# A hybrid decoder layer on one core: more sevenfold chunks in the down projection, their right-hand sums made partly in DRAM

## Chip, core and metric

The kernel runs on one core of a Trainium2 chip. The metric is the device time of one execution in microseconds; 2% is about what a measurement of this kernel can tell from no change.

## The reference

One decoder layer on 256 tokens of width 2048 in float32. A mixer joins a gated recurrence (RG-LRU) and a sliding-window attention with sinks (32 query heads, 4 key heads of 64), an output projection follows, and then an MLP with hidden width 8192. Cut to what matters:

```python
h = rmsnorm(x, norm_mix_pre[l])
proj = h @ w_in[l]                               # xr, yr, q, k, v and two gates
...
scores = jnp.einsum('bnqhgd,bnkhd->bnhgqk', qb, kk).astype(jnp.float32)
...
mix = sigmoid(g_rnn) * (y_rnn @ w_rnn_proj[l]) + sigmoid(g_attn) * (y_att @ w_attn_proj[l])
x = x + rmsnorm(mix @ w_out[l], norm_mix_post[l])
h = rmsnorm(x, norm_mlp_pre[l])
u = jnp.square(jax.nn.relu(h @ w_mlp_up[l]))     # 2048 -> 8192
x = x + rmsnorm(u @ w_mlp_down[l], norm_mlp_post[l])   # 8192 -> 2048
```

## The kernel before

**Three products for one.** Every weight and activation is split into a high part in the reduced-precision type fp32r and a low part, what the rounding left. A product is three matmuls: high by high, high by low, low by high (`product`, L905 to L908).

**The stream.** All weights come through one `Stream`: 1 MiB chunks of 128x2048 float32, in halves of 1024 columns. The SP queue loads a half into one of four raw buffers (L73), ScalarE copies the high part (`whi`, L91), VectorE subtracts to get the low part (`wlo`, L92), and TensorE uses both. There are six buffers of each part, and the splits are written six halves ahead of use. The order of the program text sets the order; a scheduler then places each engine's instructions.

**The MLP.** The hidden width is done in two halves f = 0, 1. The up phase of a half makes 16 blocks of hidden columns (`a_pair`, L234 for the high part of the weights, L237 for the low), each from two chunks. `evacuate` squares them. The down phase follows (`down`), two passes n = 0, 1 over 1024 output columns each, 16 chunks p = 0 to 15 a pass, in eight banks of PSUM: four that exist only for the sevenfold products (`P1`, `P6`, `Q5`, `N7`, in two two-bank tiles `s0` and `s1` that the up phase uses too) and four `P2`, `Q3`, `Q4`, `Cs`.

**Sevenfold chunks.** A chunk p covers 2x2 blocks of weights and 2x2 of activations. Done plainly, that is 8 block products, 24 matmuls of 128x512. For p in `SEVEN` = 0, 2, 4, ..., 12 it is done in 7 block products (Strassen's scheme in Winograd's form), 21 matmuls. It needs sums of the blocks on both sides. The left-hand sums are made once when the hidden block is evacuated (`seven`). The right-hand sums of the weights are made in each pass by VectorE in `split_sums` (L104, L106, L107), and need a split of their own (L110 on ScalarE, L111 on VectorE). Seven chunks in four passes are 28.

**Scores.** `attention` computes the scores of the four heads of one parity, which lie on 64 partitions, into one bank (two banks where the keys are 256 wide), and then those of the other parity, on the other 64 partitions (L527); VectorE empties each bank (L532).

Of the kernel before, what the change touches and what calls it, by code (L numbers as in the profile page):

```python
# [34 lines left out]
WRAW, WHALF, T2, HELD = 4, 6, 8, 4  # L35

SEVEN = (0, 2, 4, 6, 8, 10, 12)
PAIRS = 16
# [13 lines left out]
class Stream:  # L52
# [3 lines left out]
    def __init__(self, nc, pool, chunks, room, sums):  # L56
        self.nc, self.pool, self.chunks, self.room, self.sums = nc, pool, chunks, room, sums
        self.raw, self.parts = {}, {}
        self.loaded = self.split = 0
        self.pin = lambda i: i  # L60
        self.at = 0

    def load_to(self, n):
        while self.loaded < min(n, 2 * len(self.chunks)):
            j = self.loaded
            c = slice(j % 2 * 1024, j % 2 * 1024 + 1024)
            if j < 2 * EXTRA:
                if j % 2 == 0:
                    self.place = self.room(f"wraw{j}")
                t = self.place[:, c]  # L70
            else:
                t = self.pool.tile([P, 1024], F32, tag="wraw", bufs=WRAW, name=f"wraw{j}")
            self.nc.sync.dma_start(t, self.chunks[j // 2][:, c])  # L73
            self.raw[j] = t
            self.loaded += 1

    def split_to(self, n):
        while self.split < min(n, 2 * len(self.chunks)):
            j = self.split
            if j // 2 in self.sums:  # L80
                self.split_sums(j)
                self.split += 2
                continue
            self.load_to(j + 1)
            self.parts[j] = self.two_parts(self.raw.pop(j), j)
            self.split += 1

    def two_parts(self, src, j):
        hi = self.pool.tile([P, 1024], F32R, tag="whi", bufs=WHALF, name=f"whi{j}")
        lo = self.pool.tile([P, 1024], F32R, tag="wlo", bufs=WHALF, name=f"wlo{j}")  # L90
        self.pin(self.nc.scalar.copy(hi, src))  # L91
        self.pin(self.nc.vector.tensor_tensor(lo, src, hi.bitcast(F32), ALU.subtract))  # L92
        return hi, lo

    def split_sums(self, j):


        self.load_to(j + 2)
        v = self.nc.vector
        a, b = self.raw.pop(j), self.raw.pop(j + 1)  # L100
        t = self.room(f"t{j}")[:, 0:1536]
        hi, lo = [self.room(f"t{part}{j}").bitcast(F32R)[:, 0:1536] for part in ("hi", "lo")]
        one, two, l, r = t[:, 0:1024], t[:, 1024:1536], slice(0, 512), slice(512, 1024)
        v.tensor_tensor(one.rearrange("p (a b) -> p a b", a=2), b[:, l].unsqueeze(1).to_broadcast([P, 2, 512]),  # L104
                        a.rearrange("p (a b) -> p a b", a=2), ALU.add)
        v.tensor_tensor(b[:, l], t[:, l], a[:, r], ALU.add)  # L106
        v.tensor_tensor(two, b[:, l], b[:, r], ALU.add)  # L107
        ahi, alo = self.two_parts(a, j)
        bhi, blo = self.two_parts(b, j + 1)
        self.nc.scalar.copy(hi, t)  # L110
        v.tensor_tensor(lo, t, hi.bitcast(F32), ALU.subtract)  # L111
        parts = {"B11": (ahi[:, l], alo[:, l]), "B22": (ahi[:, r], alo[:, r]), "T2": (bhi[:, l], blo[:, l]),
                 "B21": (bhi[:, r], blo[:, r])}
        for i, name in enumerate(("T1", "T3", "T4")):
            c = slice(i * 512, i * 512 + 512)
            parts[name] = hi[:, c], lo[:, c]
        self.parts[j] = parts

    def ahead(self, j):
        self.split_to(j + AHEAD)  # L120
        self.load_to(max(2 * EXTRA, j + WHALF) + WRAW)

    def half(self, run_ahead=True):
        j = self.at
        self.at += 1
        if run_ahead:
            self.ahead(j)
        else:
            self.split_to(j + 1)
        return self.parts.pop(j)  # L130

    def seven(self):

        j = self.at
        self.at += 2
        self.ahead(j)
        return self.parts.pop(j)
# [4 lines left out]
AHEAD = 6  # L142
HELD_LAST = 5
# [6 lines left out]
def layer(tc, x, pos_t, pos_row, inv_freq, vecs, sinks, gains, w_kv, w_q, w_xy, w_rg, w_g, w_rp, w_ap, w_out,  # L150
# [9 lines left out]
    pairs = [psa, psa]  # L160

# [22 lines left out]
    chunks += [w_out[i] for i in range(16)]  # L184
    sums = set()
    for f in range(2):
        chunks += [w_up[32 * f + i] for i in range(32)]
        for n in range(2):
            sums.update(len(chunks) + i for i in SEVEN)
            chunks += [w_dn[(2 * f + n) * PAIRS + i] for i in range(PAIRS)]  # L190

# [6 lines left out]
    ws = Stream(nc, wpool, chunks, lambda name: flat(unit(name, F32)), sums)  # L198
# [25 lines left out]
    def a_pair(acts, out):  # L224
# [3 lines left out]
        for f in range(2):  # L228
            both = ps[:, f].rearrange("p a b -> p (a b)")
            for half in range(2):  # L230
                hi, lo = ws.half()
# [4 lines left out]
                for k, a in enumerate(act):  # L236
                    mm(ps[:, f, 1, :], lo[:, k * P : k * P + P], a[:, 0, :], start=False,  # L237
                       stop=half == 1 and k == 7)
# [889 lines left out]
```

## Time and profile before

| | us |
|---|---|
| runs | 1554.41, 1555.5, 2158.74 (median 1555.5) |
| profiled execution | 1553.58 |
| its span | 1551.8 |
| TensorE busy | 1525.7 (98%) |
| VectorE busy | 1117.5 (72%) |
| ScalarE busy | 843.9 (54%) |
| GpSimd busy | 1.7 |
| high parts, L91, 528 instructions | 549.0 |
| low parts, L92, 528 instructions | 639.8 |

The span is what the profiler recorded between the first and the last instruction; 1.8 us lie around it. Busy times of different engines overlap. The up phases run from 850 to 1030 us and from 1197 to 1375, the down phases from 1030 to 1197 and from 1375 to 1543. In rows of the profile PE is TensorE, PEld its weight load, DVE VectorE, ACT ScalarE, POOL GpSimd and SP the queue that loads the weights; L908 is line 908 of the kernel.

### The profile page before, as it was taken

Reading aid. Unit: us, or ns where it says so; the run is one execution under the profiler, and the core shown is the slowest. Engines: PE = TensorE matmul, PEld = TensorE weight load, DVE = VectorE, ACT = ScalarE, POOL = GpSimd, SP = SyncE. Lnnn points to the kernel's source line nnn. Section 1 sums busy time; section 2 is a strip of 40 time slices with the busy share of each in tenths; the row PEclk is TensorE's granted clock in tenths of the full one; section 3 lists DMA queues with packets and bytes.
Section 4 is the critical chain, followed back from the end, with each engine's and each line's share of the span. In section 5 each row is a group of like instructions: output and inputs, shape, how many; then the busy total and the mean of one; then the engine's idle time right before and its main releaser. Section 6 shows DMA issues by size and latency. Waiting matters only on the chain.

```text
span 1551.8 us, 20974 instructions
## 1 busy us (share of the span) xinstructions
PE 1525.7 (98%) x8042; PEld 1295.5 (83%) x8042; DVE 1117.5 (72%) x1364; ACT 843.9 (54%) x1156; POOL 1.7 (0%) x9
## 2 busy tenths in 40 slices
PE   8999999999999999999999999999999999999997
PEld 6887777888888888888787888888888888888885
DVE  6666666866859877555655866688886666788997
ACT  5555545646647766444344655555454555555553
POOL 0000000000000000000000000000000000000000
PEclk9999999999999999999999999999999999999999
DMA  6554354354655465555663855556666655566664
GB/s 246 188 169 148 115 173 147 124 191 149 229 188 177 158 213 198 190 184 190 250 221 98 278 190 189 187 175 213 218 203 218 221 187 189 188 242 232 203 216 138
DMA packets 82902, 296.26 MB, mean 191 GB/s; under 512 B 9585, under 2 KB 9841, under 8 KB 81777
## 3 DMA queue, kind: packets, MB, share of 16 engines
q1 hardware_dynamic: 79344, 285.48, 55.7%
q10 hardware_dynamic: 3458, 9.45, 1.6%
q8 instruction: 63, 1.03, 0.3%
q14 instruction: 37, 0.30, 0.1%
HBM read 288.60 MB, written 6.29 MB: 190 GB/s over the span
## 4 chain that ended last, share of the span: by engine, by line
PE 87%; DVE 5%; ACT 3%; DMA 3%; issue 2%; SPq 0%; DVEq 0%; ACTq 0%
PE ps L234 36%; PE ps L237 18%; PE dQ L908 7%; PE s L908 4%; PE dP L908 3%; DVE wlo L92 2%; PE dCs L908 2%; DMA wraw<-in_w_dn 2%; PE o L251 2%; PE o L255 2%; PE o L253 2%; PE q L251 2%; PE q L253 2%; PE q L255 2%; PE sc L527 1%
## 5 line engine op out<-in xcount | busy, mean ns | idle before, releaser
L92 DVE TENSOR_TENSOR wlo<-wraw,whi 128x1024 fp32r<-128x1024 f32 x528 | 639.8, 1221 | 322.4 <-ACT whi L91 317.0
L91 ACT CAST whi<-wraw 128x1024 fp32r<-128x1024 f32 x528 | 549.0, 1049 | 585.9 <-PE ps L234 271.5
L234 PE MATMUL ps<-hT,whi 128*128 128x512 f32 x1024 | 260.5, 394 | 0.0
L234 PE MATMUL ps<-h2T,whi 128*128 128x512 f32 x1024 | 258.2, 394 | 0.5 <-DVE h2T L280 0.5
L234 PEld LDWEIGHTS ps<-hT,whi 128*128 128x128 f32 x1024 | 183.8, 189 | 36.5 <-issue 3.5
L234 PEld LDWEIGHTS ps<-h2T,whi 128*128 128x128 f32 x1024 | 185.3, 190 | 34.2 <-DVE h2T L280 0.9
L237 PEld LDWEIGHTS ps<-hT,wlo 128*128 128x128 f32 x1024 | 140.1, 190 | 11.7 <-issue 2.0
L237 PEld LDWEIGHTS ps<-h2T,wlo 128*128 128x128 f32 x1024 | 140.0, 191 | 10.1
L237 PE MATMUL ps<-hT,wlo 128*128 128x256 f32 x1024 | 145.3, 283 | 0.0
L237 PE MATMUL ps<-h2T,wlo 128*128 128x256 f32 x1024 | 143.0, 283 | 0.0
L908 PE MATMUL dQ<-whi,uT 128*128 128x512 f32 x288 | 106.5, 389 | 0.0
L234 PE MATMUL ps<-yrnn,whi 128*128 128x512 f32 x256 | 64.4, 393 | 0.7 <-DVE yrnn L700 0.7
L234 PE MATMUL ps<-yatt,whi 128*128 128x512 f32 x256 | 64.1, 392 | 0.0
L908 PEld LDWEIGHTS dQ<-whi,uT 128*128 128x128 f32 x288 | 54.1, 188 | 11.2
L908 PE MATMUL dQ<-wlo,uT 128*128 128x512 f32 x144 | 56.1, 390 | 1.6 <-DVE wlo L92 1.6
L111 DVE TENSOR_TENSOR tlo<-t,thi 128x1536 fp32r<-128x1536 f32 x28 | 49.2, 1757 | 10.1 <-ACT thi L110 10.1
L908 PE MATMUL dP<-whi,uT 128*128 128x512 f32 x144 | 53.8, 389 | 0.0
L908 PE MATMUL dCs<-whi,uT 128*128 128x512 f32 x144 | 53.7, 389 | 0.0
L234 PEld LDWEIGHTS ps<-yrnn,whi 128*128 128x128 f32 x256 | 46.0, 189 | 9.3 <-DVE yrnn L700 1.1
L234 PEld LDWEIGHTS ps<-yatt,whi 128*128 128x128 f32 x256 | 46.0, 189 | 8.2
L251 PE MATMUL q<-whi,hT 128*128 128x512 f32 x128 | 51.1, 399 | 0.0
L253 PE MATMUL q<-wlo,hT 128*128 128x512 f32 x128 | 50.2, 392 | 0.0
(251 smaller groups left out, 2068.6 us busy)
## 6 DMA issues: line engine op xcount, KB each, us to landing
wraw<-in_w_up SPq DMA_DIRECT2D x128, 512.0 KB, 4.6
wraw<-in_w_dn SPq DMA_DIRECT2D x128, 512.0 KB, 4.5
wraw<-in_w_g SPq DMA_DIRECT2D x64, 512.0 KB, 4.4
wraw<-in_w_xy SPq DMA_DIRECT2D x64, 512.0 KB, 3.9
wraw<-in_w_q SPq DMA_DIRECT2D x32, 512.0 KB, 4.3
wraw<-in_w_ap SPq DMA_DIRECT2D x32, 512.0 KB, 3.8
wraw<-in_w_rp SPq DMA_DIRECT2D x32, 512.0 KB, 4.6
wraw<-in_w_out SPq DMA_DIRECT2D x32, 512.0 KB, 4.8
```

Of the source, the lines that this page charges most:

```text
L91: self.pin(self.nc.scalar.copy(hi, src))
L92: self.pin(self.nc.vector.tensor_tensor(lo, src, hi.bitcast(F32), ALU.subtract))
L111: v.tensor_tensor(lo, t, hi.bitcast(F32), ALU.subtract)
L234: mm(both, hi[:, k * P : k * P + P], a.rearrange("p a b -> p (a b)"), start=half == 0 and k == 0, stop=False)
L237: mm(ps[:, f, 1, :], lo[:, k * P : k * P + P], a[:, 0, :], start=False, stop=half == 1 and k == 7)
L251: mm(banks[tb][n], a[:, 0, t], hi[:, n * 512 : n * 512 + 512], start=first, stop=False)
L253: mm(banks[tb][n], a[:, 0, t], lo[:, n * 512 : n * 512 + 512], start=False, stop=False)
L255: mm(banks[tb][n], a[:, 1, t], hi[:, n * 512 : n * 512 + 512], start=False, stop=last)
L527: mm(ps[:, i * w : i * w + w], qT[r0 : r0 + HD, h, tb * P : tb * P + P], kT[r0 : r0 + HD, g, 0:w], start=True, stop=True)
L908: mm(b, a[x], w[y], start=not begun and i == 0, stop=tail and i == 2)
```

## The change

There are seven parts.

1. **42 sevenfold chunks.** `SEVEN` becomes a table for each half f: ten chunks a pass for f = 0 and eleven for f = 1, so 2 × 10 + 2 × 11 = 42. Chunk 0 is plain in every pass.
2. **Sums in DRAM.** For 28 of the 42, GpSimd's queue makes the four right-hand blocks in a DRAM tile: three copies and three accumulating transfers, 2 MiB written for a chunk. A step is issued with every sixth piece that isn't of the down weights. The other 14 (`MAKE`: p = 2, 6, 10, 13 for f = 0, p = 2, 5, 9 for f = 1) are made by VectorE.
3. **Pieces for halves.** The stream works in pieces of up to 2048 columns: two raw buffers (two more from the pool `big` at the start and in the down phases), three pairs of high and low parts. A sevenfold chunk is two pieces: a, three blocks of the weights (1536 columns), loaded; and b, the four sums (2048 columns), loaded from DRAM or made. The products follow them, three blocks and then four.
4. The last `a_pair` of an up phase is emptied with priority.
5. **Scores.** The products of the two parities alternate, each parity in its own bank.
6. Three (f = 0) or four (f = 1) of the `seven` tiles lie in the pool `big`.
7. In the last pass `x1` is loaded later, the gain `g3` comes before the pass on ScalarE's queue, and its products with `acc` are made after chunks 2 to 5.

```diff
-WRAW, WHALF, T2, HELD = 4, 6, 8, 4
-SEVEN = (0, 2, 4, 6, 8, 10, 12)
+T2, HELD = 8, 2
+SEVEN = ((1, 2, 3, 5, 6, 7, 9, 10, 11, 13), (1, 2, 3, 4, 5, 7, 8, 9, 10, 11, 12))
+MAKE = ((2, 6, 10, 13), (2, 5, 9))
+IN_UNITS = (3, 4)
...
+            if self.pieces[j][0] is None and c.start == 0:
+                self.make(src, self.free(j - 1))
+            hi, lo = self.parts[j]
+            i = self.pin(self.nc.scalar.copy(hi[:, c], src[:, c]))
+            self.pin(self.nc.vector.tensor_tensor(lo[:, c], src[:, c], hi[:, c].bitcast(F32), ALU.subtract))
...
+    def make(self, t, w):
         v = self.nc.vector
+        q = [slice(i * 512, i * 512 + 512) for i in range(4)]
+        v.tensor_tensor(t[:, 0:1024].rearrange("p (a b) -> p a b", a=2), w[:, q[3]].unsqueeze(1).to_broadcast([P, 2, 512]),
+                        w[:, 0:1024].rearrange("p (a b) -> p a b", a=2), ALU.add)
+        v.tensor_tensor(t[:, q[2]], t[:, q[0]], w[:, q[1]], ALU.add)
+        v.tensor_tensor(t[:, q[3]], t[:, q[2]], w[:, q[2]], ALU.add)
...
+PARTS, RAW = 3, 2
+EVERY = 6
...
+                    if i in MAKE[f]:
+                        pieces.append((piece(src)[0], 1536, 2048, own(at)))
+                        pieces.append((None, 2048, 2048, own(at + 1)))
+                    else:
+                        t = away.tile([P, 2048], F32, name=f"sums{len(ahead_of)}")
+                        ahead_of.append((t, src))
+                        pieces.append(piece(src, 1536, 2048, own(at)))
+                        pieces.append(piece(t, 2048, 2048, own(at + 1)))
...
+            if i >= 2:
+                t, w = ahead_of[i - 2]
+                dma(t[:, 1536:2048], t[:, 1024:1536], accum_op=ALU.add)
+            if 1 <= i <= len(ahead_of):
+                t, w = ahead_of[i - 1]
+                dma(t[:, 1024:1536], t[:, 0:512], accum_op=ALU.add)
+            if i < len(ahead_of):
+                t, w = ahead_of[i]
+                dma(t[:, 0:512], w[:, 1536:2048])
+                dma(t[:, 512:1024], w[:, 1536:2048])
+                dma(t[:, 1024:2048], w[:, 512:1536])
+                dma(t[:, 0:1024], w[:, 0:1024], accum_op=ALU.add)
+            yield step
...
+        if j % EVERY == 0 and j >= EVERY and pieces[j][0] and pieces[j][0][0][1].tensor.name != w_dn.tensor.name:
+            for d in next(summing, ()):
+                tc.add_manual_dep(d.ins, i.ins.name, after, reason="a step of the sums")
...
-            for par in range(2):
-                r0 = par * HD
-                for j in range(4 // per):
-                    ps = bank(psm, "sc")
-                    for i in range(per):
-                        h = j * per + i
-                        mm(ps[:, i * w : i * w + w], qT[r0 : r0 + HD, h, tb * P : tb * P + P],
+            for j in range(4 // per):
+                both = [bank(psm, "sc") for par in range(2)]
+                for i in range(per):
+                    h = j * per + i
+                    for par in range(2):
+                        r0 = par * HD
+                        mm(both[par][:, i * w : i * w + w], qT[r0 : r0 + HD, h, tb * P : tb * P + P],
                            kT[r0 : r0 + HD, g, 0:w], start=True, stop=True)
...
+    LEFT = {"P1": (0, 0), "Q3": (6, 1), "P2": (2, 2), "Q5": (4, 0), "N7": (3, 1), "P6": (5, 2), "Q4": (1, 3)}
...
-            a_pair(h2T, wide(u))
+            a_pair(h2T, wide(u), PRIO if p == PAIRS - 1 else 0)
```

Three places show what the new text makes of the engines' order. The first is TensorE in the attention: the scores of one group (`sc` are the banks, `kT` and `qT` the keys and queries), before and then now; `ps` and `q10` are other projections.

```order
L527 MATMUL sc_912<-kT_428,qT0_816 128x128 x4
L527 MATMUL sc_919<-kT_428,qT0_816 128x128 x4
...
L527 MATMUL sc_1064<-kT_428,qT0_816 128x256 x2
L527 MATMUL sc_1069<-kT_428,qT0_816 128x256 x2
L251 MATMUL q10_1077<-whi32_888,hT0_138 128x512
```

```order
L582 MATMUL sc_900<-kT_437,qT0_813 128x128
L582 MATMUL sc_901<-kT_437,qT0_813 128x128
L582 MATMUL sc_900<-kT_437,qT0_813 128x128
L582 MATMUL sc_901<-kT_437,qT0_813 128x128
...
L582 MATMUL sc_1021<-kT_437,qT0_813 128x256 x2
L582 MATMUL sc_1046<-kT_437,qT0_813 128x256 x2
L307 MATMUL q10_1059<-whi16_934,hT0_166 128x512
L582 MATMUL sc_1047<-kT_437,qT0_813 128x256 x2
```

The 128-wide products alternate between two banks. The 256-wide of this group stay in twos of one bank; in two of the four groups one pair of banks alternates.

The second is TensorE where the first down phase opens, before and then now; `ps` is the last up block.

```order
L237 MATMUL ps_9007<-h2T3_6759,wlo335_8945 128x256 x4
L908 MATMUL s0_9110<-whi336_8972,seven00_7781 128x512
L908 MATMUL s0_9110<-wlo336_8973,seven00_7781 128x512
L908 MATMUL s0_9110<-whi336_8972,seven00_7781 128x512
L908 MATMUL dQ3_9113<-whi336_8972,seven00_7781 128x512
...
L908 MATMUL dQ4_9114<-thi336_8967,seven00_7781 128x512
L908 MATMUL s1_9111<-thi336_8967,seven00_7781 128x512
```

```order
L290 MATMUL ps_8636<-h2T3_6535,wlo167_8591 128x256 x4
L971 MATMUL dQ3_8722<-whi168_8637,uT00_7182 128x512
L971 MATMUL dQ3_8722<-wlo168_8638,uT00_7182 128x512
L971 MATMUL dQ3_8722<-whi168_8637,uT00_7182 128x512
...
L971 MATMUL dCs_8724<-wlo168_8638,uT00_7182 128x512
L971 MATMUL dCs_8724<-whi168_8637,uT00_7182 128x512
L971 MATMUL s0_8719<-whi169_8674,seven01_7495 128x512
```

The two-bank tiles `s0` and `s1` were needed with the first and the sixteenth matmul of the phase; now 24 matmuls of a plain chunk come ahead of the first that needs them.

The third is VectorE where it makes sums: before, chunk 4 of the first pass and the plain one behind it, and now p = 3, 4 and 5 of the first pass of f = 1 (pieces 257 to 262, made from 261 into 262).

```order
L104 TENSOR_TENSOR t344_9163<-wraw345_9116,wraw344_9086 128x1024
L92 TENSOR_TENSOR wlo344_9170<-wraw344_9086,whi344_9169 128x1024
L106 TENSOR_TENSOR wraw345_9116<-t344_9163,wraw344_9086 128x512
L107 TENSOR_TENSOR t344_9163<-wraw345_9116 128x512
L92 TENSOR_TENSOR wlo345_9174<-wraw345_9116,whi345_9173 128x1024
L92 TENSOR_TENSOR wlo346_9217<-wraw346_9147,whi346_9216 128x1024
L92 TENSOR_TENSOR wlo347_9221<-wraw347_9149,whi347_9220 128x1024
L111 TENSOR_TENSOR tlo344_9165<-t344_9163,thi344_9164 128x1536
```

```order
L103 TENSOR_TENSOR wlo257_11390<-wraw257_11321,whi257_11389 128x1536
L103 TENSOR_TENSOR wlo258_11406<-wraw258_11324,whi258_11405 128x2048
L103 TENSOR_TENSOR wlo259_11423<-wraw259_11371,whi259_11422 128x1536
L103 TENSOR_TENSOR wlo260_11439<-wraw260_11374,whi260_11438 128x2048
L117 TENSOR_TENSOR wraw262_11409<-wraw261_11393 128x1024
L103 TENSOR_TENSOR wlo261_11458<-wraw261_11393,whi261_11457 128x1536
L119 TENSOR_TENSOR wraw262_11409<-wraw262_11409,wraw261_11393 128x512
L120 TENSOR_TENSOR wraw262_11409<-wraw262_11409,wraw261_11393 128x512
L103 TENSOR_TENSOR wlo262_11471<-wraw262_11409,whi262_11470 128x2048
```

A made sum was followed by the parts of a plain chunk ahead of its own last part; now two chunks without adds stand ahead of the three adds, and the part of piece 262 directly behind them. GpSimd, which issued no transfers, now issues all those of part 2.

More of the change, by code (lines that the diff above doesn't have):

```diff
@@ L119, in ahead, with load @@
[L119 to L123, printed above, removed]
+        self.each = lambda j, i: None
+        self.waits = [0, 0]
+    def load(self):
+        if self.loaded == len(self.pieces):
+            return False
+        j = self.loaded
+        loads, w, step, own = self.pieces[j]
+        if self.waits[own] == (EXTRA if j < EXTRA else RAW):
+            return False
+        t = self.room(f"wraw{j}") if own else self.pool.tile([P, 2048], F32, tag="wraw", bufs=RAW, name=f"wraw{j}")
+        for c, src in loads or ():
+            self.nc.sync.dma_start(t[:, c], src)
+        self.raw[j] = t
+        self.waits[own] += 1
+        self.loaded += 1
+        return True
@@ L124, in half, with ahead, next @@
+    def ahead(self, last):
+        self.split_to(sum(j <= last for j, c in self.cuts))
+        while self.load():
+            pass
+    def next(self, run_ahead=True):
         j = self.at
         self.at += 1
[L126 to L136, printed above, removed]
+        self.ahead(j + PARTS - 1 if run_ahead else j)
         return self.parts.pop(j)
```

303 lines of the change are left out of this document (152 added, 151 removed).

## The prediction

> **What bounds the kernel now.** I read the page's totals first, then the chain, the waits, and the work stage by stage.
>
> ```profile
> PE 1525.7 (98%) x8042; PEld 1295.5 (83%) x8042; DVE 1117.5 (72%) x1364; ACT 843.9 (54%) x1156; POOL 1.7 (0%) x9
> PE 87%; DVE 5%; ACT 3%; DMA 3%; issue 2%; SPq 0%; DVEq 0%; ACTq 0%
> ACT whi L91 <- PE ps L234: 271.5, 195, 4.1
> DVE wlo L92 <- ACT whi L91: 317.0, 294, 3.0
> ```
>
> TensorE is busy for 98% of the span and carries 87% of the chain that ended last. The two largest waits show the direction: the split of a weight into high and low part starts on ScalarE when TensorE gives a buffer back, and VectorE follows ScalarE. The feeders wait for TensorE, so only matmul time comes off the end, and a feeder costs something only once it is late.
>
> ```profile
> core 0: us, PE busy (x) PEld busy (x) DVE busy (x) ACT busy (x) POOL busy (x), PEclk, DMA share, GB/s
> 850.00:1030.00 180.00, 180.00 (x1024) 158.23 (x1023) 132.79 (x166) 104.31 (x140) 0.00 (x0) 0.99 0.62 205
> 1030.00:1197.00 167.00, 166.21 (x736) 137.44 (x736) 138.18 (x132) 85.56 (x82) 0.00 (x0) 1.00 0.62 209
> 1197.00:1375.00 178.00, 178.00 (x1023) 156.69 (x1022) 124.17 (x147) 97.09 (x119) 0.00 (x0) 1.00 0.60 195
> 1375.00:1543.00 168.00, 165.26 (x728) 135.90 (x726) 144.94 (x148) 84.43 (x92) 0.00 (x0) 1.00 0.64 215
> ```
>
> The rows are the up and down phases of the two halves of the hidden layer. TensorE is full in all four, and the clock is at 0.99 to 1.00, so nothing is to be had from the clock. In the down phases VectorE is at 83% and 86% already: it is the feeder with the least left. The profiled execution took 1553.6 us (span 1551.8 and 1.8 around it), 0.1% under the median of 1555.5. The sum below starts from 1553.6.
>
> **(a) Fewer products.** A plain chunk needs 24 matmuls, a sevenfold one 21. With 42 sevenfold chunks for 28, 14 × 3 = 42 matmuls of 128x512 go.
>
> ```profile
> 1447.98 2.72 PE dQ L908 x12
> 999.99 1.84 PE ps L234 x8
> 1001.83 0.95 PE ps L237 x8
> ```
>
> In the chain twelve down matmuls take 2.72 us, 0.227 each: 42 × 0.227 = −9.5 us. The same price gives what is needed later: a plain chunk holds TensorE for 5.44 us, a sevenfold one for 4.76, now in two pieces, a (9 matmuls, 2.04) and b (12, 2.72). An up chunk is 2 × (1.84 + 0.95) = 5.58.
>
> **(b) Scores.** The two head parities lie on the upper and lower 64 partitions; their products now alternate between two banks.
>
> ```profile
> L527 PE MATMUL sc<-kT,qT 64*128 64x256 f32 x64 | 17.0, 396 | 0.0
> L527 PE MATMUL sc<-kT,qT 64*128 64x128 f32 x64 | 6.8, 285 | 0.0
> L567 PE MATMUL po<-pT,v_sb 128*64 128x512 f32 x32 | 7.7, 605 | 0.0
> L339 PE MATMUL gain_b<-gain,ones 128*128 128x512 f32 x8 | 3.7, 609 | 0.3 <-DMA gain<-in_gains 0.3
> ```
>
> No row shows 64-row products side by side. The nearest do so for columns: the 32 po records, which use 64 columns each and alternate between the halves, hold TensorE for 7.7/32 = 0.24 us each, the full-width records of the same length 3.7/8 = 0.46. So two halves did run together, and I take half the time where the instructions really alternate. In the changed order all of the 128-wide products alternate, but of the 256-wide only those of the second bank pair in two of the four groups, a quarter: −6.8/2 − 17.0/8 = −5.5 us. Bounds: 0 if nothing overlaps, −11.9 if all does.
>
> The Trainium skill's "TensorEngine Tiling (Array Packing)", section "Performance Considerations", says against this that tiling speeds up the matmuls but not what empties PSUM. The row on it in this trace is the next one, VectorE's emptying of the score bank: TensorE waited for it once, 0.4 us. By the rule taken fully this term would be 0 and the sum 1555; the trace speaks for the row.
>
> ```profile
>   DVE s L532: 0.4, 1
> ```
>
> **(c) Opening of the down phase.** Today it opens with a sevenfold chunk, whose products need the two-bank tile that the last up chunk still occupies.
>
> ```profile
> 1034.94 0.50 PE L908 MATMUL s<-thi,seven 128*128 128x512 f32 x1 [0.79 <-DVE u L241]
> 1379.68 0.50 PE L908 MATMUL s<-thi,seven 128*128 128x512 f32 x1 [1.12 <-DVE u L241]
> ```
>
> These are TensorE's gaps of 0.79 and 1.12 us. A plain chunk first gives 5.44 us of work in other banks, and the last up tile is emptied with priority: −1.9 us (0 if another wait takes the place).
>
> **(d) Sums on VectorE.** Fourteen sevenfold chunks still make their sums there, and now without half the buffers: three pairs of high and low parts, each a whole piece.
>
> ```profile
> L92 DVE TENSOR_TENSOR wlo<-wraw,whi 128x1024 fp32r<-128x1024 f32 x528 | 639.8, 1221 | 322.4 <-ACT whi L91 317.0 <-issue 3.6 <-PE ps L237 0.7
> L111 DVE TENSOR_TENSOR tlo<-t,thi 128x1536 fp32r<-128x1536 f32 x28 | 49.2, 1757 | 10.1 <-ACT thi L110 10.1
> L104 DVE TENSOR_TENSOR t<-wraw,wraw 128x1024 f32<-128x1024 f32 x28 | 34.2, 1223 | 9.9 <-DMA wraw<-in_w_dn 9.2 <-PE dQ L908 0.3
> L106 DVE TENSOR_TENSOR wraw<-t,wraw 128x512 f32<-128x512 f32 x28 | 19.2, 684 | 0.1
> L107 DVE TENSOR_TENSOR t<-wraw 128x512 f32<-128x512 f32 x28 | 19.3, 691 | 0.9
> L91 ACT CAST whi<-wraw 128x1024 fp32r<-128x1024 f32 x528 | 549.0, 1049 | 585.9 <-PE ps L234 271.5 <-DVE wraw L106 66.7 <-issue 52.3
> L110 ACT CAST thi<-t 128x1536 fp32r<-128x1536 f32 x28 | 41.4, 1479 | 14.6 <-DVE t L107 8.3 <-PE s L908 6.2
> ```
>
> No row has 2048 columns; one step further from 1024 and 1536 gives 1.76 + 0.54 = 2.29 us on VectorE and 1.48 + 0.43 = 1.91 on ScalarE. A chunk whose sums VectorE makes costs it 1.22 + 0.68 + 0.69 + 1.76 + 2.29 = 6.64 us against 4.76 of TensorE, 1.88 too much; one whose sums come from DRAM 4.05, a plain one 2.29 against 5.44. On average VectorE keeps up, but it may be only three pieces ahead. Take p = 5 of the second half, after two DRAM chunks. Time 0 is when TensorE has done piece a of p = 3. ScalarE and VectorE split piece b of p = 4 (1.91, 2.29: 4.20), then VectorE does three adds and the low part of piece a (4.35: 8.55); piece b of p = 5 is copied (10.46) and subtracted (12.75). TensorE has b, a, b, a before it: 2.72 + 2.04 + 2.72 + 2.04 = 9.52. It stalls 3.2 us. So does p = 9, in both passes: 4 × 3.2 = +12.9 us. The other ten follow a plain chunk among the last two (10.20 + 2.04 = 12.24 against 12.75, or more room): 0.5 us each at most, within the overlap of neighbouring instructions, taken as 0. Bounds: 0, and 14 × 1.88 = 26.3.
>
> The 14 additional (pass, chunk) places are 7 more chunks whose activations are spread into seven; their added VectorE work (three small subtractions and three more column blocks) lies in the up phases, where VectorE idles for about 50 us each: 0.
>
> **(e) Loads in the down phase.** A DRAM chunk loads 0.75 + 1 MiB (1.835 MB) in 4.76 us: 385 GB/s wherever such chunks follow each other.
>
> ```profile
> 16.00:22.00 6.00, 5.77 (x22) 4.55 (x21) 4.53 (x8) 3.40 (x10) 0.00 (x0) 0.62 1.03 411
> 1375.00:1400.00 25.00, 23.88 (x107) 19.43 (x106) 16.87 (x17) 12.22 (x13) 0.00 (x0) 1.00 0.87 318
> wraw<-in_w_dn SPq DMA_DIRECT2D x128, 512.0 KB, 4.5
> ```
>
> The fullest stretch moved 411 GB/s; the second row, 318 at a share of 0.87, makes 366 when full. At 366 a DRAM chunk takes 5.01 us, 0.25 more than TensorE: 28 × 0.25 = 7 us at most. I take 0: runs are two or three long, and a plain chunk or a stall of (d) follows each. A transfer lands 4.5 us after its issue, which two pieces ahead cover.
>
> **(f) Sums in DRAM.** GpSimd's queue, idle today, issues a step each six pieces, mostly before the down phases: 1 MiB copied and 1 MiB added, with the reading of the old value about 3 MiB of traffic, on the transfer engines that carry the weights. On average it fits: six up pieces (6.29 MB) and a step (3.15) are 9.44 MB in 6 × 5.58 = 33.5 us, 282 GB/s. At 366 GB/s one step is 8.6 us. If all of it went ahead of the loads, the split pieces in hand cover 2 × 5.58 − (1.91 + 2.29) = 6.96 us, and 1.6 us stay uncovered: 0 to 28 × 1.6 = 45 us. I take 0, since the loads are issued in the same time and share the engines. The two raw buffers in front also count: a load of 5 us, copy and subtraction make 9.2 us for two chunks of 11.2, so a load may be 2 us late.
>
> **Sum.** 1553.6 − 9.5 − 5.5 − 1.9 + 12.9 = 1549.6, given as 1550 us.
>
> **The rivals.**
> 1. *VectorE is never late.* If the adds slip into VectorE's waits for ScalarE, (d) is 0: 1553.6 − 16.9 = 1537 us, with all scores halved 1530. For it: VectorE waited 317 us for ScalarE. Against it: the adds stand in order behind the subtraction of the piece before.
> 2. *The down phases become feeder-bound*, on the other side of the time before. It decides from the point where VectorE, at 83 to 86% today, has no slack that it can use before a made sum, and DRAM chunks run at 366 GB/s: 1553.6 − 16.9 + 26.3 + 7 = 1570 us. Against it: ten of the made sums stand near a plain chunk.
> 3. *GpSimd's transfers starve the weights.* It decides once a step holds up a load by more than 6.96 us: 1549.6 + 45 = 1594 us, with TensorE gaps each six pieces in the up phases. For it: the transfer engines are at 0.60 to 0.62 there without any steps. The Trainium skill's "DMA: Bandwidth & Descriptors", section "Issuing engines are not separate DMA queues", states that transfers from different engines end on the same 16 and interleave; by that rule the delay is shared, not whole, and no run here has shown it.
>
> **How the numbers follow.** Forecast 0.45; rival 1 0.25; rival 2 0.18; rival 3 0.12. A measurement of this kernel tells about 2% from no change, 1524 and 1587 us. Faster by over 2% needs all of rival 1 and full scores and something more: 0.03. Slower by over 2% is rival 3 nearly alone: 0.11. The rest is 0.86. The range leaves out rival 3 and a little of rival 1: from 1529 (rival 1 with all scores) to 1572 (rival 2 and 2 us); the forecast's own is 1540 to 1560.
>
> **What would show it.** TensorE with 42 fewer records of 128x512 in the down phases; no gap at their opening; the 128-wide scores near 0.05 us each; gaps of about 3 us before the fourth to seventh product (the sums' piece) of p = 5 and 9 in the second half, released by VectorE's low part; none elsewhere. I am wrong if those gaps are missing (then 1537), if gaps stand before pieces that a load releases, or if the up phases grow beyond 180 us.

## The result, and the profile after

The changed kernel takes 1658.97 us (median of 4 runs, 1650.47 to 1664.7) against 1554.95 before: 1.067 times, interval 1.061 to 1.073. It is slower, and outside the forecast range of 1529 to 1572 us. The run of 2158.74 us before stands apart from the others and isn't in the ratio. The profiled execution has a span of 1659.2 us.

First the totals, the queues and the chain from the profile page of the changed kernel (a queue's row has its packets, the MB that it moved and its share of the 16 transfer engines):

```profile
PE 1552.2 (94%) x8000; PEld 1302.9 (79%) x8000; DVE 1102.7 (66%) x1236; ACT 844.2 (51%) x1049; POOL 117.5 (7%) x177
q1 hardware_dynamic: 87120, 306.45, 53.8%
q0 software_dynamic: 20608, 58.73, 18.3%
PE 39%; DMA 30%; DVE 16%; ACT 9%; issue 4%; SPq 1%; DVEq 0%; ACTq 0%
```

TensorE executes 42 records fewer and is busy 26.5 us longer; it idles for 107 us, against 26 before. Transfers, 3% of the chain before, are 30% now. The new queue `q0` is GpSimd's: it moved 58.73 MB in 18.3% of what the 16 transfer engines have, 304 us or 10.8 us for each of the 28 steps, 193 GB/s counted by the bytes written; the weights' queue `q1` moved 306 MB in 53.8%, 343 GB/s.

The span cut into stages, in us, each cut at the first matmul of the next stage (the last four columns are experiments below):

| stage | before | after | no transfers | halves | halves, no transfers | halves, placed |
|---|---|---|---|---|---|---|
| start | 66.5 | 66.1 | 65.8 | 66.1 | 65.4 | 67.4 |
| queries, attention | 255.2 | 266.2 | 253.2 | 256.1 | 251.8 | 251.8 |
| attention projection | 139.7 | 139.7 | 139.7 | 139.7 | 139.7 | 139.9 |
| recurrence and gates | 128.9 | 155.0 | 129.1 | 143.9 | 128.9 | 128.9 |
| recurrence projection | 157.4 | 161.3 | 158.0 | 157.6 | 157.6 | 157.6 |
| output projection | 101.7 | 118.3 | 104.9 | 107.5 | 101.3 | 101.4 |
| up, first half | 181.1 | 209.1 | 181.0 | 185.1 | 179.3 | 182.4 |
| down, first half | 165.7 | 171.4 | 164.0 | 162.8 | 160.5 | 162.1 |
| up, second half | 178.7 | 178.8 | 178.7 | 178.8 | 178.7 | 178.7 |
| down, second half | 168.1 | 184.5 | 184.4 | 161.1 | 160.6 | 161.8 |
| tail | 8.7 | 8.8 | 8.8 | 9.7 | 9.6 | 9.7 |

Two stages side by side tell most. The up phases do the same work; 5 of GpSimd's steps fall into the first and a last transfer into the second, and only the first lost time, 28 us. In the windows of the changed kernel (the columns as in the prediction):

```profile
472.00:627.04 155.04, 134.06 (x786) 119.59 (x786) 110.51 (x145) 102.03 (x151) 16.54 (x24) 0.92 0.74 214
906.64:1115.71 209.07, 190.32 (x1029) 165.45 (x1029) 125.58 (x137) 98.35 (x109) 20.67 (x30) 0.93 0.80 233
1287.13:1465.88 178.75, 178.75 (x1025) 157.31 (x1024) 119.45 (x123) 91.38 (x90) 0.84 (x1) 1.00 0.60 200
1465.88:1650.35 184.47, 171.12 (x704) 133.83 (x702) 143.86 (x109) 95.62 (x72) 0.00 (x0) 0.96 0.74 263
```

The first row (gates) and the second (up, first half) have 21 and 19 us of idle TensorE, and a clock of 0.92 and 0.93. The last row (down, second half) shows a second loss, 13 us idle in a stage without any of GpSimd's transfers.

TensorE's gaps in the timeline of the changed kernel, the longest one of each of four stages (in brackets the length of the gap and what ended it):

```profile
546.67 0.58 PE L725 MATMUL pg<-xs,whi 128*128 128x256 f32 x1 [10.98 <-ACT room L730]
799.25 1.22 PE L303 MATMUL o<-whi,mixT 128*128 128x512 f32 x2 [10.72 <-DVE pp L294]
1091.62 3.74 PE L288 MATMUL ps<-h2T,whi 128*128 128x512 f32 x8 [5.92 <-DVE u L294]
1490.62 0.50 PE L971 MATMUL s<-whi,seven 128*128 128x512 f32 x1 [3.84 <-ACT whi L102]
```

None names a transfer. The one at 1091.62 waits for `u`, the emptying of a two-bank tile, but the chain through it starts with a transfer:

```profile
1058.21 1.91 ACT whi L102
1060.14 2.30 DVE wlo L103
1062.46 0.33 SPq L84
1062.83 5.12 DMA wraw<-in_w_up
1068.06 1.92 ACT whi L102
1070.00 2.30 DVE wlo L103
1072.32 0.33 SPq L84
1072.69 13.95 DMA wraw<-in_w_up
1086.74 1.91 ACT whi L102
1088.67 2.29 DVE wlo L103
1090.97 0.61 DVE u L294
1091.62 1.65 PE ps L288 x3
```

A weight load issued at 1072.69 landed after 13.95 us. ScalarE's copy and VectorE's subtraction waited for it, and the emptying of a finished tile, whose input had long been there, stood behind them in VectorE's order. The rows above it show the ring of the raw buffers: a load is issued when VectorE has done with a whole buffer, and ScalarE's next copy waits until the whole piece is there. From one copy to the next this took 9.85 us, for two up chunks that hold TensorE for 5.58 us each. What GpSimd did then, and the queues between 1070 and 1092 us (packets, MB, share of the 16 engines):

```profile
1071.51 2.17 POOL L227 DMA_DIRECT2D sums<-in_w_dn  x3
q0 software_dynamic: 722, 2.06, 61.0%
q1 hardware_dynamic: 640, 2.29, 29.1%
```

It issued a step just before the load. In 22 us its 2.06 MB took 61% of the engines, while 2.29 MB of weights took 29%. The load got almost nothing at first: of what began between 1072 and 1077 us, GpSimd's queue has all (102.6% of the engines, as its packets run on past the end of the window) and the weights' queue 0.4%; from 1077 to 1087 us they have 50.5 and 47.5%.

Behind the gap TensorE is slow too. Windows over it and behind it, clock in the third column from the right:

```profile
1091.00:1094.00 3.00, 2.38 (x6) 1.92 (x7) 2.96 (x3) 2.35 (x3) 0.00 (x0) 0.50 0.86 171
1094.00:1097.00 3.00, 3.00 (x16) 2.59 (x15) 1.10 (x2) 0.00 (x0) 0.00 (x0) 0.80 0.96 324
1097.00:1100.00 3.00, 3.00 (x19) 2.62 (x18) 0.00 (x0) 1.36 (x1) 0.00 (x0) 1.00 0.74 261
```

After 5.9 us of standing still the granted clock is 0.50, and full again after about 3.6 us of work (0.80 in the second row is 1.2 us at half and 1.8 us at full clock). The slow clock is where TensorE's additional busy time comes from. The Trainium skill's "TensorE: Matmul & The Clock Gate", section "Part 1: The HAM clock gate (the "warmup" mystery)", states that an idle array falls to half its clock and needs some 3.4 us of work to be released; the three rows agree.

### The profile page after: what moved, and what is told of

The parts are those of the page before. It is cut to its first block, busy times and chain, and to the rows that moved or that the text cites. A ratio compares the mean times of both kernels' runs of the same rounds, so it can differ in the third digit from the quotient of the medians.

```text
span 1659.2 us, 20585 instructions
## 1 busy us (share of the span) xinstructions
PE 1552.2 (94%) x8000; PEld 1302.9 (79%) x8000; DVE 1102.7 (66%) x1236; ACT 844.2 (51%) x1049; POOL 117.5 (7%) x177
## 3 DMA queue, kind: packets, MB, share of 16 engines
q1 hardware_dynamic: 87120, 306.45, 53.8%
q0 software_dynamic: 20608, 58.73, 18.3%
HBM read 369.34 MB, written 65.01 MB: 262 GB/s over the span
## 4 chain that ended last, share of the span: by engine, by line
PE 39%; DMA 30%; DVE 16%; ACT 9%; issue 4%; SPq 1%; DVEq 0%; ACTq 0%
PE ps L288 13%; DVE wlo L103 9%; ACT whi L102 7%; PE ps L290 6%; DMA wraw<-in_w_up 6%; DMA wraw<-in_w_rp 4%; DMA wraw<-in_w_xy 4%; DMA wraw<-in_w_g 4%; PE dQ L971 3%; DMA wraw<-in_w_dn 3%; DMA wraw<-in_w_ap 2%; PE s L971 2%; DMA wraw<-sums 2%; DMA wraw<-in_w_out 2%; DMA wraw<-in_w_rg 2%
## 5 line engine op out<-in xcount | busy, mean ns | idle before, releaser
L103 DVE TENSOR_TENSOR wlo<-wraw,whi 128x1024 fp32r<-128x1024 f32 (+2 forms) x442 | 689.8, 1582 | 422.2 <-ACT whi L102 416.1
L102 ACT CAST whi<-wraw 128x1024 fp32r<-128x1024 f32 (+2 forms) x442 | 583.0, 1338 | 579.7 <-DMA wraw<-in_w_up 91.6
L971 PE MATMUL s<-whi,seven 128*128 128x512 f32 x336 | 120.8, 401 | 7.0 <-ACT whi L102 7.0
L227 POOL DMA_DIRECT2D sums<-in_w_dn x112 | 82.7, 988 | 339.5 <-DMA sums<-in_w_dn 294.8
L227 POOL DMA_DIRECT2D sums<-sums x56 | 46.9, 953 | 835.5 <-ACT whi L102 835.4
L971 PEld LDWEIGHTS s<-whi,seven 128*128 128x128 f32 x336 | 65.1, 195 | 22.3 <-ACT whi L102 9.1
L971 PE MATMUL s<-wlo,seven 128*128 128x512 f32 x168 | 69.4, 413 | 7.2 <-DVE wlo L103 6.8
L971 PE MATMUL dQ<-whi,seven 128*128 128x512 f32 x168 | 66.1, 397 | 1.0 <-ACT whi L102 1.0
L971 PE MATMUL dQ<-whi,uT 128*128 128x512 f32 x176 | 64.7, 395 | 0.9 <-ACT whi L102 0.8
L303 PE MATMUL o<-whi,mixT 128*128 128x512 f32 x128 | 44.9, 411 | 13.2 <-DVE pp L294 10.7
```

The lines of the kernel that those rows point to most:

```text
L102: i = self.pin(self.nc.scalar.copy(hi[:, c], src[:, c]))
L103: self.pin(self.nc.vector.tensor_tensor(lo[:, c], src[:, c], hi[:, c].bitcast(F32), ALU.subtract))
L227: step.append(nc.gpsimd.dma_start(*args, **how))
L303: mm(banks[tb][n], a[:, 0, t], hi[:, n * 512 : n * 512 + 512], start=first, stop=False)
L971: mm(b, a[x], w[y], start=not begun and i == 0, stop=tail and i == 2)
```

## The experiments

Theory A is that GpSimd's transfers alone are the cost. Rival B is that the new stream's buffers are too short by themselves. Rival C, which came later, is that it takes both. In the runs without transfers the 28 sums from DRAM are left out and blocks of the weights are loaded in their place, so these two kernels (whole pieces and halves), and those built on them, don't compute the layer.

### Without the transfers, and spread out

```diff
-                        t = away.tile([P, 2048], F32, name=f"sums{len(ahead_of)}")
-                        ahead_of.append((t, src))
-                        pieces.append(piece(t, 2048, 2048, own(at + 1)))
+                        pieces.append(piece(src, 2048, 2048, own(at + 1)))
```

> The changed kernel without any of GpSimd's transfers. Where a piece of sums came from DRAM, the chunk's own four weight blocks are loaded instead (the same bytes, the same number of loads), so the sums of 28 chunks are left out and the output is not the layer's. Theory A (the 28 steps on GpSimd's queue slow the weight loads; everything outside the down phases that was lost is theirs): the stages before the down phases return to their times before (up phase of the first half 181 us, not 209; the stretch with the gates 129, not 155; the output projection 101, not 118), the granted clock returns to above 0.99, and the time is 1559 to 1572 us. Rival B (the stream itself is too short: two raw buffers of a whole piece instead of four halves, three part buffers instead of six): time stays above 1630 us, with the same gaps.

Measured: 1567.36 us, 1.008 times before (1.005 to 1.010). The transfers cost 91.6 us here, every stage ahead of the down phases but the output projection is back, and the clock is at 0.99. Theory A holds for these stages, as far as it says that nothing is lost without the transfers. But 12 us over the time before stay. The last down phase alone is 16 us longer (184.4 us), where the forecast had the time fall; the output projection has 3 us more, and the other stages together are shorter.

```diff
-EVERY = 6
+EVERY = 1
-            yield step
+            for d in step:
+                yield [d()]      # one transfer, issued when its turn comes
```

> The same transfers on GpSimd's queue, all 168, but one with every piece of the stream instead of six with every sixth. Theory A1 (it is the burst: six transfers in front of the next loads make one load later than the about 7 us that the split pieces cover): a load meets one transfer of 256 or 512 KB, TensorE's gaps outside the down phases mostly go, time 1565 to 1590 us. Theory A2 (it is the volume: the transfers take 300 us of all 16 engines wherever they stand): 1640 to 1670 us. Rival B (stream too short) also expects no change, about 1659.

Measured: 1625.75 us, 1.045 (1.043 to 1.048), between the two forms of A: spread, the same transfers cost 58 us, not 92. So the burst is a part of the cost and not all of it.

### Copies instead of accumulations

```diff
-                dma(t[:, 0:1024], w[:, 0:1024], accum_op=ALU.add)
+                dma(t[:, 0:1024], w[:, 0:1024])
```

and so for the two other accumulations.

> The changed kernel with all of GpSimd's transfers as plain copies, none accumulating; the sums are left out, their places hold copies, and the output is not the layer's. As many transfers, as many bytes written. If cost goes by bytes moved (an accumulation reads one operand more, so 3 MiB read or written a step fall to 2): the queue's share falls from 18.3% to about 12% and the time to 1610 to 1635 us. If accumulating itself is slow: share below 9%, time below 1600. If the DRAM-to-DRAM packet is what costs: share and time stay, 1645 to 1660.

Measured: 1620.18 us, 1.042 (1.040 to 1.045). The page's row for the queue:

```profile
q0 software_dynamic: 17024, 58.73, 13.6%
```

13.6% of 1618.2 us is 220 us of the engines, against 304, or 0.72 of it. By the text of the kernel a step with accumulations reads 3 MiB (its old values among them) and writes 2, and without them it reads 2 and writes 2: 0.67 of the bytes read, 0.80 of all. The time lies between, so the bytes explain most of the difference; a small price of accumulating by itself isn't excluded, as the page doesn't count the old values (369.34 MB read from memory in both kernels). The results of this kernel are not the layer's.

### The scores and the opening alone, in the kernel before

```diff
-            for par in range(2):
-                r0 = par * HD
-                for j in range(4 // per):
+            for j in range(4 // per):
+                both = [bank(psm, "sc") for par in range(2)]
...
-SEVEN = (0, 2, 4, 6, 8, 10, 12)
+SEVEN = (1, 3, 5, 7, 9, 11, 13)     # only in the second of the two
```

> The kernel before with the interleaved scores alone. By the forecast's price 5.5 us less, 1549 us. By the stage of the run without transfers, where queries and attention took 253.2 us and not 255.2, 2 us less, about 1553 us. If interleaving does nothing: 1555.

> The kernel before with the interleaved scores and with its 28 sevenfold chunks at p = 1, 3, ..., 13, so that each pass opens with a plain chunk (the last pass holds two chunks back, not three). The stream is the old one. If the opening's gaps of 0.79 and 1.12 us go, 1.9 us under the run with the scores alone; if another wait takes their place (the chunk behind the sevenfold one, or the later end of the sums at the last pass), the same or more.

Measured: 1550.16 us, 0.997 (0.996 to 0.999) for the scores, 4.0 us less, between the two prices; and 1550.6, 0.998 (0.997 to 0.999) with the opening, which brought nothing more: the openings' gaps are gone, but the tail after the last matmul grew from 8.7 to 12.3 us. The last sevenfold chunk now ends nearer to the end, and one chunk fewer is held back; which of the two lengthens the tail was not tried. The two groups of score products in the first of these kernels:

```profile
L527 PE MATMUL sc<-kT,qT 64*128 64x256 f32 x64 | 13.6, 402 | 0.0
L527 PE MATMUL sc<-kT,qT 64*128 64x128 f32 x64 | 4.6, 285 | 0.0
```

The 128-wide, which alternate fully, fall from 6.8 to 4.6 us: by a third, not by half. The start times in the traces show why. Where they alternate, two products start within 7 ns of each other, and such a pair follows each 0.11 us, as a single one did before, so two halves do run together. But before, three pairs of a group's 16 products had coincided already, and the first step of a group takes 0.21 us in both kernels. A group falls from 1.71 to 1.16 us. Of the 256-wide products about half alternate in this kernel and a quarter in the changed one, so the row falls from 17.0 to 13.6 us here and to 15.0 there.

### The last down phase

```diff
-        for tb in range(TB):
-            nc.scalar.dma_start(acc[tb], acc_away[tb])
+            if p in (2, 5, 6, 9):
+                tb, i = divmod((2, 5, 6, 9).index(p), 2)
+                c = quarter(2 * n + i)
+                    nc.scalar.dma_start(acc[tb][:, c], acc_away[tb][:, c])
```

> The changed kernel without GpSimd's transfers (as in the first experiment, sums left out), and with the 2 MiB of the first half's result (acc) loaded in quarters of 256 KB through the last two passes instead of all at the opening of the second half's down phase. If that load is what makes p = 4 late there (it took 14 us, and the next weight load was issued behind it in time), the gaps of 3.5 and 1.0 us at p = 4 and the low clock behind them go, and the second down phase falls from 184 to 176 to 179 us; time 1559 to 1563. Rival (two raw buffers and VectorE's adds cannot feed this phase, whatever else is loaded): 184 us and 1567 stay.

Measured: 1565.76 us, 1.008 (1.006 to 1.009), no difference to the run without transfers that the times can show. In the profiles the last down phase falls from 184.4 to 180.2 us, less far than the 176 to 179 expected, and the gaps of 3.5 and 1.0 us are gone, so this load was their cause, but it is a small part. What stays are the stalls behind VectorE's adds. ScalarE's and VectorE's rows and TensorE's two gaps, at p = 5 of the first pass:

```profile
1401.81 0.69 DVE L120 TENSOR_TENSOR wraw<-wraw,wraw 128x512 f32<-128x512 f32 x1
1402.62 5.08 ACT L102 CAST whi<-wraw 128x2048 fp32r<-128x2048 f32 x3 [3.97 <-DVE wraw L120]
1404.57 0.74 PE L969 MATMUL s<-whi,seven 128*128 128x512 f32 x2 [1.22 <-ACT whi L102]
1406.37 0.50 PE L969 MATMUL dQ<-whi,uT 128*128 128x512 f32 x1 [0.83 <-ACT whi L102]
```

The place and the chain are the forecast's: adds, then a copy of 2048 columns, then the sums' piece. But the copy's high part releases TensorE, not VectorE's low part: TensorE starts with products of the high part while the low part is still made, and the size is 2.05 us, not 3.2. The four places together have 6.8 us of the 10.95 that TensorE idles in this stage; the rest are smaller gaps at sevenfold chunks.

### All sums on VectorE, with whole pieces

```diff
-SEVEN = ((1, 2, 3, 5, 6, 7, 9, 10, 11, 13), (1, 2, 3, 4, 5, 7, 8, 9, 10, 11, 12))
-MAKE = ((2, 6, 10, 13), (2, 5, 9))
+SEVEN = ((1, 3, 5, 7, 9, 11, 13), (1, 3, 5, 7, 9, 11, 13))
+MAKE = SEVEN
```

> The new stream, scores and opening, but 28 sevenfold chunks as before, at p = 1, 3, 5, ..., 13, all their sums made on VectorE, none in DRAM (the last pass holds two chunks back, not three, and the spread activations lie all in their own pool). The whole layer is computed. Theory A: no gap outside the down phases, and in the down phases each made chunk stands behind a plain one; TensorE's work is that of before, so 1553.6 - 4.2 for the scores - 1.9 at the opening = 1548, plus up to 2.5 us of stall at each made chunk, 1548 to 1610, nearer the low end. Rival B: the up phases stay at 209 and 180 us, above 1600 us through them.

Measured: 1579.26 us, 1.016 (1.013 to 1.018). The up phases took 180.7 and 178.8 us, so B falls as a cause of the loss there; the down phases took 171.0 and 187.7. So the new stream is late in the down phases even with no transfers on GpSimd's queue.

### The same transfers in the old stream

GpSimd's steps were added to the kernel before, at the same chunks; nothing reads what they make.

```diff
+        if j % 12 == 1 and j >= 12 and j // 2 not in downs:
+            for d in next(summing, ()):
+                tc.add_manual_dep(d.ins, i.ins.name, after, reason="a step of the sums")
```

> The kernel before, unchanged in its 28 sevenfold chunks and in its stream of halves (four raw buffers of 512 KB, six halves split ahead), with GpSimd's 28 steps of transfers added at the same chunks; nothing reads their results. Theory A (the transfers alone are the cost): as much as between the changed kernel and its version without them, 92 us, so 1630 to 1650. Rival C (it takes both: the old stream, with its finer buffers, would have carried the transfers, and the new one of whole pieces cannot): less than 30 us, 1555 to 1585.

> The same transfers added to the kernel before, one with every chunk instead of six with every sixth. In the new stream spreading brought the cost from 92 us down to 58. Theory A: about 58 here too, 1600 to 1620. Rival C: close to nothing, 1555 to 1570.

Measured: 1581.08 us, 1.018 (1.015 to 1.020) in bursts; 1573.31, 1.011 (1.009 to 1.014) spread. The same transfers cost 27 and 19 us here, against 92 and 58. That speaks for C and against A alone, though the spread form is 3 us above C's range.

### Halves in the new stream

Every piece is kept in two halves, each in a buffer of its own, with the same bytes in all; each is loaded, split and given back by itself.

```diff
-        t = self.room(f"wraw{j}") if own else self.pool.tile([P, 2048], F32, tag="wraw", bufs=RAW, name=f"wraw{j}")
+            t = self.pool.tile([P, 1024], F32, tag="wraw", bufs=2 * RAW, name=f"wraw{j}h{h}")
...
-                self.parts[j] = [self.pool.tile([P, 2048], F32R, tag=tag, bufs=PARTS, name=f"{tag}{j}")
+                t.tiles.append(self.pool.tile([P, 1024], F32R, tag=tag, bufs=2 * PARTS, name=f"{tag}{j}h{h}"))
```

> The changed kernel, all of it computed, with every piece of the stream kept in two halves of 1024 columns: four raw buffers of 512 KB instead of two of 1 MiB, six half-wide buffers of each part instead of three, every copy and subtraction over at most 1024 columns, each half loaded and given back by itself. The same bytes of buffers, the same 28 steps of transfers in bursts. In the old stream of halves the same steps cost 27 us, in the new one 92. Theory C (it is the grain of the buffers: a whole piece comes free, is loaded and is split late): the cost falls to 25 to 45 us over the run without transfers, 1585 to 1610. Theory D (it is something else of the new stream, such as how far the order of the program runs ahead): 1645 to 1660.

> The same halves without GpSimd's transfers (sums of 28 chunks left out, the chunk's own blocks loaded in their place). With whole pieces 1567. Theory C: the stalls of the last down phase shrink too, since copies of 1.0 us and subtractions of 1.2 take the place of 1.9 and 2.3 in the chain from the adds to the products: 1548 to 1560. Theory D: 1563 to 1570.

> Halves, and one transfer of GpSimd's with every piece instead of six with every sixth; the whole layer. Theory C: 1565 to 1585, the best form of the changed kernel, still not under the time before. Theory D: about 1620, as with whole pieces.

Measured: 1571.44 us, 1.011 (1.007 to 1.014) with bursts; 1537.33, 0.989 (0.987 to 0.992) without transfers; 1556.44, 1.002 (1.000 to 1.004) spread. Halving the buffers takes 87.5 us off the changed kernel and 30 us off the one without transfers; all three times lie below the ranges of C. The loads are held up with halves too: in the first up phase 17 of the weight loads took over 10 us from issue to landing with whole pieces and 18 with halves (at most 17.3 and 16.7 us), and without transfers none over 8.5. TensorE's idle time there is what differs, 18.8 us with whole pieces and 1.9 with halves. Raw buffers and part buffers were halved together, so which of them counts more is open. The down phases in the run without transfers:

```profile
1024.13:1184.64 160.51, 160.51 (x711) 132.89 (x709) 139.25 (x144) 99.26 (x108) 0.00 (x0) 1.00 0.77 264
1363.38:1523.98 160.60, 160.04 (x704) 131.34 (x702) 145.56 (x159) 101.97 (x123) 0.00 (x0) 1.00 0.82 296
```

TensorE is busy in all of the first and all but 0.6 us of the second, and VectorE makes the same 14 chunks of sums as with whole pieces.

### Where the rest of the transfers' cost lies

```diff
-        if j % EVERY == 0 and j >= EVERY and pieces[j][0] ...
+        if j >= EVERY and not 68 <= j < 92 and pieces[j][0] ...
```

> Halves, one transfer with every piece, but none with the 24 pieces 68 to 91, the stretch of the recurrence's gates; the whole layer. In the run with halves and spread transfers that stretch took 141.9 us against 128.9 without transfers, 13 of the 17 us that its profile had left over. Theory C1 (what is left of the cost stands where other work of ScalarE is queued behind a late split, so it depends on the place): 1553 - 13 = 1538 to 1546 us, under the time before. Theory A2 (volume: the same 300 us of transfer engines cost the same wherever they stand): 1553 to 1560.

> Halves, 28 sevenfold chunks at p = 1, 3, ..., 13, all sums made on VectorE, no transfers on GpSimd's queue (the last pass holds two chunks back); the whole layer. With whole pieces this was 1579, its down phases 171.0 and 187.7 us. Theory C (grain of the buffers): the down phases fall to about 165 each (the 728 matmuls of one take 165), the rest as in the run with halves without transfers, 1541 to 1548 us. Theory B2 (VectorE cannot make sums behind every plain chunk): 1560 or more.

Measured: 1543.0 us, 0.993 (0.992 to 0.995), with the transfers kept away from the gates; 1549.02, 0.997 (0.996 to 0.999), with all 28 sums on VectorE, where the down phases took 164.6 and 167.2 us, 171.0 and 187.7 with whole pieces. The gates' stretch in the first of them, with one of GpSimd's transfers left in it, and the recurrence projection behind it:

```profile
459.19:588.07 128.88, 128.86 (x787) 114.87 (x787) 104.12 (x139) 97.88 (x146) 0.52 (x1) 1.00 0.53 173
588.07:745.68 157.61, 156.91 (x898) 137.42 (x896) 97.18 (x100) 77.65 (x89) 20.09 (x29) 1.00 0.93 271
```

The gates are back at their time; the projection behind them takes 29 transfers at a share of 0.93 and loses nothing. So what was left of the cost depends on the place. In the gates ScalarE and VectorE are busy for 76 and 81% of the time, and work that TensorE needs is queued behind each split; that this is why just they are sensitive was not tried. The kernel with halves and placed transfers computes the whole layer. It is far faster than the changed kernel, and 0.7% faster than the one before: clear of no change by its interval, but under the 2% named at the start.

What the transfers cost, in us, as differences of the medians. The 5.7 compares two rounds, in which the kernel before had 1552.35 and 1554.25 us; with that difference taken out it is 7.6.

| stream | bursts | spread | spread, none at the gates |
|---|---|---|---|
| old, halves | 26.7 | 18.9 | not run |
| new, whole pieces | 91.6 | 58.4 | not run |
| new, halves | 34.1 | 19.1 | 5.7 |

Three whole raw buffers, which would have told their number from their grain, were not tried.

## Why the prediction was wrong

**The step that failed is (f), GpSimd's transfers, taken as 0 with 45 us as the bound.** They cost 91.6 us: TensorE idles 64.5 us more than in the run without them (107.0 and 42.5) and is busy 27 us longer. Rival 3 named the mechanism, with a chance of 0.12, and its price was too low by half. Three things were priced wrongly. The forecast's own sign of being wrong, an up phase beyond 180 us, came with 209.

- *The cover.* The forecast took the two split pieces in hand, 6.96 us, as what a late load can use up. It named the ring of two raw buffers too (9.2 us for two chunks of 11.2), but didn't use it in the price. That ring is what the chain shows: 9.85 us a turn, which leaves 1.3 us to make up what a step has cost, and a load that landed 9.2 us later than the median (13.95 and 4.8) left TensorE standing for 5.9. The same bytes in halves bring the cost to 34 us, although the loads are as late there. The forecast listed the change from halves to pieces as part 3 of the change and gave it no term.
- *The step.* It was priced at 8.6 us from 3.15 MB at 366 GB/s; it took 10.8 us of all 16 engines. The forecast took 0 because loads and step share the engines. That the queues' transfers interleave, which the Trainium skill states in the section quoted with rival 3, holds in much of the trace: while the load ahead of the gap at 546.67 was under way (533 to 545 us) the two queues had 49.8 and 49.1% of the engines, and that load still took 11 us. For the load shown above it does not hold in the first four us or so, when the step had all of the engines. Shared or not, the load was late.
- *The clock.* A gap was priced by its own length. TensorE's busy time grew by 27 us between the run without transfers (1525.2) and the changed kernel (1552.2), at a clock of 0.99 and 0.965.

**(a) Fewer products: right.** With halves and without transfers the down phases fall by 5.2 and 7.5 us; 18 and 24 matmuls at 0.227 us and the gaps at the openings make 4.9 and 6.6.

**(b) Scores: −5.5 forecast, −4.2 in the rows of the changed kernel.** The 256-wide products give 2.0 us there, as forecast (2.1); the 128-wide 2.2 instead of 3.4, since part of them had run together already and a group's first step doesn't shrink. The kernel with the scores alone alternates more of them, so its −4.0 us (interval −5.9 to −2.2) is no measure of this term, and doesn't exclude −5.5.

**(c) Opening: right in the trace,** both gaps are gone. By itself, in the old stream, it showed no gain in the time.

**(d) Sums on VectorE: right in place, nearly right in the chain,** 6.8 us at four places for 12.9. But the stage lost more than that: without transfers it took 180.2 us with whole pieces, `acc` already loaded later, and 160.6 with halves. Of the 19.6 us, 10.4 are idle time and 9.2 slower matmuls, at a clock of 0.98, which the forecast had not counted. That the stalls were the price of whole pieces, and not of VectorE, it had not seen: at p = 5 of the first pass the runs with halves have 0 to 1.2 us left.

**(e) Loads in the down phase: taken as 0.** The run of two DRAM chunks behind the opening met the 2 MiB of `acc` and lost 4.5 us; the forecast had looked at the weights alone.

So rivals 1 and 2 each had a part. Without transfers the kernel with whole pieces stands at 1567, near rival 2's 1570, but by luck in the number: only the second down phase was longer, and part of that was `acc` and the clock. With halves it stands at 1537, where rival 1 had put the changed kernel, and there VectorE is hardly ever late; but it is another kernel than the one forecast.

## What to carry to other kernels

A prefetch is as deep as the smallest unit that can come free: two buffers of 1 MiB were worth much less than four of 512 KB (30 us without background transfers, 87.5 with them), and the difference shows where something delays a load or a split: in the up phases without transfers it was under 2 us. To price a late load, take the time of one turn of the buffer ring from its rows, and what it leaves beside the work that it feeds. Before adding transfers that run in the background, look for stretches whose feeders have slack, not at the mean share of the transfer engines, and add the slow clock behind each gap to its price. Follow a gap on the chain further back than its releaser: none of the four gaps shown here named a transfer, and the chain of each began with one, three times a weight load of 9.7 to 14 us and once the load of `acc`.

## What had not been expected of the hardware

By the bytes written and the time that their packets took, transfers from DRAM to DRAM moved 193 GB/s with the accumulations, and 267 (58.73 MB in 220 us) as plain copies, both beside weight loads, where the loads beside the first moved 343. Products on different halves of the rows, where they alternated, ran as pairs: two started within 7 ns, and a pair took the 0.11 us that one of them takes alone. Those on different halves of the columns took about half of a full one each (0.24 for 0.46). A TensorE gap of 5.9 us was followed by 3.6 us at half clock.
